# The chunked scan of a hybrid trunk: the state product from two-part operands, and first and last chunks with fewer products

## The chip, the cores and the metric

The kernel runs on one core of a Trainium2 chip. The metric is the device time of one execution in microseconds (us). The engines in the profile are PE (TensorE, matmuls; PEld is its weight load), DVE (VectorE), ACT (ScalarE), POOL (GpSimd) and SP (SyncE, which issues the DMAs).

## The reference

One layer of a trunk over 2048 positions of width 1024, in float32. A normalised input goes through one input projection. Part of its columns feed a short gated convolution, the others a state-space scan (SSD); both are concatenated, projected back and added to the input. A squared-ReLU MLP and a final normalisation follow. The part that matters here is the scan, with 16 heads of 64 in two groups that share B and C (state size 128):

```python
states = einsum("bclgn,bclgrp->bcgrpn", b_c, x_c * decay_end[..., None])
chunk_decay = exp(a_cum[:, :, -1:])
def step(hs, inp):
    s_c, d_c = inp
    return hs * d_c[..., None, None] + s_c, hs
h0 = zeros((b, g, r, p, n))
_, prev = lax.scan(step, h0, (states, chunk_decay))
y_off = einsum("bclgn,bcgrpn->bclgrp", c_c, prev) * exp(a_cum)[..., None]
return y_diag + y_off
...
y = y + d_skip[:, None] * xs
gated = rmsnorm(y * silu(z), norm_w)
```

`y_diag` is the part within a chunk, from scores and decays; `y_off` is what the state before the chunk adds. The state starts at zero, and nobody reads the state after the last chunk.

## The kernel before

The kernel works on chunks of 128 positions. There are 4 blocks `b` of 512 positions, each with 2 groups `g` and 4 chunks `c`: 32 chunks in the order of `CHUNKS`, block by block, group by group. Chunks 0 to 15 (`sp1`, `bufs` of 1) run beside the second half of the input projection (`second_half`, whose matmuls are on lines 267 to 269 into `px`, `py` and `pw`). Chunks 16 to 31 (`sp2`, `bufs` of 2) run beside the output projection (`unit`, whose matmuls are those of `mm3`, lines 110 to 112, into `pm`). After them come the MLP's two projections, which the change does not touch.

The large matmuls already use two-part operands: ACT rounds a tile to float32r (`whi`, line 101; `uh`), DVE subtracts that from the full value (`wlo`, line 102; `ul`), and `mm3` adds up three products hi·hi, hi·lo, lo·hi. The weights `wraw` are loaded by SP (line 96) and split so.

A chunk of the scan goes in these steps.

- `load` and `load_rows`: SP loads B and C (`bc`, line 1184), the inputs `xd` (line 1186), the running decays as rows copied to all partitions (`dec`, line 1188) and their exponentials (`eb`, line 1208). `load_gate` loads `silu(z)` into `y` (line 1215).
- `front`: TensorE transposes `xd` (`ptx`, line 1225) and B (`ptb`, line 1227), and multiplies B and C (line 1228). ACT copies these to `xtok` (line 1230) and `btok` (line 1232); DVE masks the scores (`smask`, line 1234). ACT makes the decays from `dec` (lines 1239 and 1240) and scales `xd` (line 1242). DVE multiplies `xtok` by the steps into `xdt` and by the decays to the chunk's end into `xde` (both line 1245, tile `stmp`), and `dec` by the mask (line 1247).
- `back`: TensorE makes `yo`, the old state by C (line 1259), `st`, the new state product of `btok` and `xde` (line 1261, one fp32 matmul of 128x512), and `yd`, the part within the chunk (line 1264). DVE updates the state (lines 1272 and 1273) and adds up the output (lines 1275 to 1280). A normalisation over the group follows (`ssq`, `pss`, `srstd`, lines 1283 to 1294), and a store to `yn_d` (line 1295).

`front` and `back` are generators. `run` takes their pieces in a written order, and one piece goes after each product of the projection (in `sp1`) or one or two at each hook of a unit (in `sp2`). Each engine executes its queue in order; the queues' order is fixed when the program is built and is not the source's: in the trace an engine has work of the next chunk ahead of work of this one. Every tile waits for the readers of the tile whose buffer it takes over.

Of the kernel before, what the change touches and what calls it, by code (L numbers as in the profile page):

```python
# [11 lines left out]
F32 = mybir.dt.float32  # L12
F32R = mybir.dt.float32r
AF = mybir.ActivationFunctionType
ALU = mybir.AluOpType

P = 128
# [3 lines left out]
NB = T // TB  # L21
L = 128
NC = TB // L
# [16 lines left out]
def trunk(ctx: ExitStack, tc: tile.TileContext, x, w_in, w_dt, w_out, w_up, w_down, cvec, hrow, out):  # L40
    nc = tc.nc
# [67 lines left out]
    def mm3(out, whi, wlo, hi, lo, k, nk):  # L109
        nc.tensor.matmul(out, whi, hi, start=(k == 0), stop=False)  # L110
        nc.tensor.matmul(out, whi, lo, start=False, stop=False)  # L111
        nc.tensor.matmul(out, wlo, hi, start=False, stop=(k == nk - 1))  # L112

    def psum(tag, name, bufs=1):
        if tag in turns:
            tag, bufs = next(turns[tag])
        return ps.tile([P, 512], F32, tag=tag, name=name, bufs=bufs)
# [1029 lines left out]
    class Scan:  # L1147
        def __init__(self, pool):
            self.state = []
            for g in range(G):  # L1150
                s0 = pool.tile([P, 512], F32, name=f"state{g}")
                nc.vector.memset(s0, 0.0)
                self.state.append(s0)

        def open(self, stack, name, bufs):
            self.sp = stack.enter_context(tc.tile_pool(name=name, bufs=1, reuse_waits="tile"))
# [4 lines left out]
            return self.sp.tile([P] + shape, F32, tag=tag, name=tag, bufs=bufs or self.bufs)  # L1161

        def tmp(self):
            return self.tile([512], "stmp", 2 + self.bufs)

        def place(self, n):
            b, g, c = CHUNKS[n]
# [3 lines left out]
        def load(self, n):  # L1171

            if n >= self.end:
                return
            b, g, c, h, ts, r0 = self.place(n)
            t = self.got[n] = {}
            if (g, c) == (0, 0) or n == self.begin:
                dd = self.tile([4, NC * 16], "dd")
                nc.sync.dma_start(dd, dt_d[b])
                self.dd = {**getattr(self, "dd", {}), b: dd}  # L1180
            t["dd"] = dd = self.dd[b]
            bc = t["bc"] = self.tile([2, L], "bc", 2)
            for i in range(2):
                nc.sync.dma_start(bc[:, i], xs_d[h][:, 8 + 2 * i + g, ts])
            t["xd"] = self.tile([4, L], "xd")
            nc.sync.dma_start(t["xd"], xs_d[h][:, 4 * g : 4 * g + 4, ts])
            t["dec"] = self.tile([HG, L], "dec")
            nc.sync.dma_start(t["dec"], rd_d[b][r0 : r0 + HG, 0, :].partition_broadcast(P))
            three = lambda i: dd[:, i].rearrange("p (c h) -> p c h", c=NC)[:, c, g * HG : (g + 1) * HG]
            heads = lambda a: a.unsqueeze(2).to_broadcast([P, HG, 64])  # L1190
            t["dt"], t["cdec"], t["dend"] = heads(three(0)), heads(three(2)), heads(three(3))
            t["a"] = dd[:, 1, r0 : r0 + HG]

        def load_rows(self, n):

            if n >= self.end:
                return
            b, g, c, h, ts, r0 = self.place(n)
            if self.bufs == 1:
                eb = self.tile([4, L], "eb", 1)  # L1200
            else:

                eb = uh.tile([P, 1, TB], F32R, tag="uh3", name="eb", bufs=4).bitcast(F32)
                eb = eb[:, 0].rearrange("p (j l) -> p j l", j=4)
            self.got[n]["eb"] = eb
            for hf in range(2):
                src = rd_d[b][r0 : r0 + HG, 1, :].rearrange("(j t) l -> t j l", t=2)[hf]
                nc.sync.dma_start(eb[hf * 64 : (hf + 1) * 64], src.partition_broadcast(64))

        def load_gate(self, n):  # L1210
# [3 lines left out]
            y = self.got[n]["y"] = self.tile([4, L], "y")  # L1214
            nc.sync.dma_start(y, sz_d[h][:, 4 * g : 4 * g + 4, ts])

        def front(self, n):

            b, g, c, h, ts, r0 = self.place(n)
            t = self.got[n]  # L1220
            bT, cT = t["bc"][:, 0], t["bc"][:, 1]
            byhead = lambda a: a.rearrange("p (h d) -> p h d", h=HG)
            pt = psum("tp", "ptx", 2)
            for j in range(4):
                nc.tensor.transpose(pt[:, j * P : (j + 1) * P], t["xd"][:, j], ident)
            pb = psum("tp", "ptb", 2)
            nc.tensor.transpose(pb[:, 0:P], bT, ident)
            nc.tensor.matmul(pb[:, P : 2 * P], bT, cT, start=True, stop=True)
            xtok = self.tile([512], "xtok", 1)
            nc.scalar.copy(xtok, pt)  # L1230
            btok = t["btok"] = self.tile([P], "btok", 1)
            nc.scalar.copy(btok, pb[:, 0:P])
            sm = self.tile([L], "smask", 1)
            nc.vector.tensor_tensor(out=sm, in0=pb[:, P : 2 * P], in1=tri, op=ALU.mult)
            yield

            dec = t["dec"]
            for i in range(HG):
                nc.scalar.activation(dec[:, i], dec[:, i], AF.Relu, bias=t["a"][:, i : i + 1], scale=-1.0)
            nc.scalar.activation(dec, dec, AF.Exp, scale=-1.0)  # L1240
            for j in range(4):
                nc.scalar.mul(t["xd"][:, j], t["xd"][:, j], col(C_D, 4 * g + j))
            for k, by in (("xdt", "dt"), ("xde", "dend")):
                t[k] = self.tmp()
                nc.vector.tensor_tensor(out=byhead(t[k]), in0=byhead(xtok), in1=t[by], op=ALU.mult)
            yield
            nc.vector.tensor_tensor(out=dec, in0=dec, in1=sm.unsqueeze(1).to_broadcast([P, HG, L]), op=ALU.mult)
            yield

        def back(self, n):  # L1250
# [3 lines left out]
            cT = t["bc"][:, 1]  # L1254
            byhead = lambda a: a.rearrange("p (h d) -> p h d", h=HG)
            state = self.state[g]
            yo = psum("yo", "yo")
            for j in range(4):
                nc.tensor.matmul(yo[:, j * L : (j + 1) * L], state[:, j * P : (j + 1) * P], cT, start=True, stop=True)
            st = psum("tp", "st", 2)  # L1260
            nc.tensor.matmul(st, t["btok"], t["xde"], start=True, stop=True)  # L1261
            yd = psum("yd", "yd")
            for i in range(HG):
                nc.tensor.matmul(  # L1264
# [4 lines left out]
                    stop=True,  # L1269
                )  # L1270
            y = t["y"]
            nc.vector.tensor_tensor(out=byhead(state), in0=byhead(state), in1=t["cdec"], op=ALU.mult)
            nc.vector.tensor_tensor(out=state, in0=state, in1=st, op=ALU.add)
            t1 = self.tmp()
            nc.vector.tensor_tensor(out=t1, in0=yo, in1=t["eb"].rearrange("p j l -> p (j l)"), op=ALU.mult)
            nc.vector.tensor_tensor(out=t1, in0=t1, in1=yd, op=ALU.add)
            yield
            t3 = t1.rearrange("p (j l) -> p j l", j=4)
            nc.vector.tensor_tensor(out=t3, in0=t3, in1=t["xd"], op=ALU.add)
            nc.vector.tensor_tensor(out=y, in0=t3, in1=y, op=ALU.mult)  # L1280
            yield
            q4 = self.tmp().rearrange("p (j l) -> p j l", j=4)
# [4 lines left out]
            yield  # L1287
            pss = psum("tp", "pss", 2) if self.bufs == 1 else psum("mw", "pss", accs["mw"])
            nc.tensor.matmul(pss[:, 0:L], ones, ssq, start=True, stop=True)
            r = self.tile([L], "srstd", 1)  # L1290
            nc.scalar.activation(r, pss[:, 0:L], AF.Sqrt, bias=eps, scale=1.0 / 512)
            nc.vector.reciprocal(out=r, in_=r)
            yield
# [339 lines left out]
```

## Time and profile before

| | |
|---|---|
| time of 3 runs | 2644.2, 2649.08, 2650.53 us; median 2649.08 |
| profiled execution | span 2642.3 us from the first to the last instruction; the page gives it no other time |
| engines busy | PE 98%, PEld 80%, DVE 74%, ACT 54%, POOL 2% |
| granted TensorE clock | 0.998 on average |
| scan's first product to its last | about 480 to 1280 us |

A line of a timeline reads: start in us from the span's beginning, duration, engine (SPq is SP's queue), line of the code, operation, output<-inputs, shapes, how many in a row; in brackets the idle time of the engine before it and what ended it. A line of a group reads: line, engine, operation, tiles, shapes and count, then busy us and mean ns of one, then the idle time before them. A line of a wait reads: who waited <- for whom: us in total, times, the longest. Matmuls are pipelined, so that their durations overlap; the distance from start to start is what one occupies.

### The profile page before, as it was taken

Reading aid. Unit: us, or ns where it says so; the run is one execution under the profiler, and the core shown is the slowest. Engines: PE = TensorE matmul, PEld = TensorE weight load, DVE = VectorE, ACT = ScalarE, POOL = GpSimd, SP = SyncE. Lnnn points to the kernel's source line nnn. Section 1 sums busy time; section 2 is a strip of 40 time slices with the busy share of each in tenths; the row PEclk is TensorE's granted clock in tenths of the full one; section 3 lists DMA queues with packets and bytes.
Section 4 is the critical chain, followed back from the end, with each engine's and each line's share of the span. In section 5 each row is a group of like instructions: output and inputs, shape, how many; then the busy total and the mean of one; then the engine's idle time right before and its main releaser. Section 6 shows DMA issues by size and latency. Waiting matters only on the chain.

```text
span 2642.3 us, 33439 instructions
## 1 busy us (share of the span) xinstructions
PE 2595.5 (98%) x12026; PEld 2121.3 (80%) x12026; DVE 1943.0 (74%) x2650; ACT 1423.9 (54%) x2150; POOL 57.4 (2%) x98
## 2 busy tenths in 40 slices
PE   7999999999999999999999999999999999999998
PEld 5778888778878888887888888788887888888887
DVE  7987676767777777758777775755558877888885
ACT  6644345777567666657326555755455444444443
POOL 0000010000000000000000000000000000000001
PEclk9999999999999999999999999999999999999999
DMA  3585444655555479967666673743448544665762
GB/s 146 192 304 187 143 144 174 205 160 168 158 167 186 153 242 273 288 205 233 212 210 215 227 277 142 250 162 140 166 144 299 160 149 153 211 209 175 243 207 72
DMA packets 284806, 511.78 MB, mean 194 GB/s; under 512 B 25312, under 2 KB 141024, under 8 KB 284640
## 3 DMA queue, kind: packets, MB, share of 16 engines
q1 hardware_dynamic: 284640, 509.65, 57.9%
q8 instruction: 94, 1.54, 0.2%
q14 instruction: 72, 0.59, 0.1%
HBM read 344.41 MB, written 165.15 MB: 193 GB/s over the span
## 4 chain that ended last, share of the span: by engine, by line
PE 64%; issue 24%; DMA 4%; ACT 3%; DVE 3%; SPq 1%; POOL 0%; POOLq 0%; DVEq 0%; ACTq 0%
PE px L267 9%; PE px L269 9%; PE px L268 9%; PE py L267 5%; PE py L269 5%; PE py L268 4%; PE pm L110 4%; PE pm L111 4%; PE pm L112 4%; PE pw L267 2%; PE pw L268 2%; PE pw L269 2%; DMA dec<-rd_d 2%; PE yd L1264 1%; PE st L1261 1%
## 5 line engine op out<-in xcount | busy, mean ns | idle before, releaser
L267 PE MATMUL px<-uh,whi 128*128 128x512 f32 x1672 | 656.9, 393 | 7.8 <-ACT pw L275 3.9
L269 PE MATMUL px<-uh,wlo 128*128 128x512 f32 x1672 | 652.0, 390 | 2.5 <-DVE wlo L102 2.5
L268 PE MATMUL px<-ul,whi 128*128 128x512 f32 x1672 | 651.9, 390 | 0.0
L102 DVE TENSOR_TENSOR wlo<-wraw,whi 128x1024 fp32r<-128x1024 f32 x230 | 233.8, 1017 | 212.0 <-ACT whi L101 203.1
L267 PEld LDWEIGHTS px<-uh,whi 128*128 128x128 f32 x1672 | 314.3, 188 | 82.7 <-DVE acc L984 7.0
L269 PEld LDWEIGHTS px<-uh,wlo 128*128 128x128 f32 x1672 | 314.3, 188 | 69.4 <-DVE wlo L102 3.3
L268 PEld LDWEIGHTS px<-ul,whi 128*128 128x128 f32 x1672 | 314.3, 188 | 63.6
L101 ACT CAST whi<-wraw 128x1024 fp32r<-128x1024 f32 x230 | 203.3, 884 | 278.3 <-PE px L268 198.0
L101 ACT CAST whi<-s 128x1024 fp32r<-128x1024 f32 x210 | 219.3, 1044 | 234.5 <-PE py L268 76.2
L267 PE MATMUL py<-uh,whi 128*128 128x512 f32 x836 | 327.3, 392 | 1.9 <-DVE acc L984 1.5
L268 PE MATMUL py<-ul,whi 128*128 128x512 f32 x836 | 325.5, 389 | 0.0
L269 PE MATMUL py<-uh,wlo 128*128 128x512 f32 x836 | 325.4, 389 | 0.0
L102 DVE TENSOR_TENSOR wlo<-s,whi 128x1024 fp32r<-128x1024 f32 x210 | 255.6, 1217 | 82.6 <-ACT whi L101 78.9
L110 PE MATMUL pm<-uh,whi 128*128 128x512 f32 (+1 forms) x648 | 251.8, 390 | 2.1 <-ACT uh L202 2.1
L111 PE MATMUL pm<-ul,whi 128*128 128x512 f32 (+1 forms) x648 | 248.9, 384 | 0.0
L112 PE MATMUL pm<-uh,wlo 128*128 128x512 f32 (+1 forms) x648 | 248.3, 383 | 0.0
L267 PEld LDWEIGHTS py<-uh,whi 128*128 128x128 f32 x836 | 157.0, 188 | 35.9 <-DVE acc L984 1.9
L269 PEld LDWEIGHTS py<-uh,wlo 128*128 128x128 f32 x836 | 156.9, 188 | 32.8
L268 PEld LDWEIGHTS py<-ul,whi 128*128 128x128 f32 x836 | 157.0, 188 | 32.3 <-issue 0.2
L267 PE MATMUL pw<-uh,whi 128*128 128x512 f32 x418 | 163.4, 391 | 0.7 <-ACT pw L275 0.7
L268 PE MATMUL pw<-ul,whi 128*128 128x512 f32 x418 | 162.8, 390 | 0.0
L269 PE MATMUL pw<-uh,wlo 128*128 128x512 f32 x418 | 162.8, 389 | 0.0
(226 smaller groups left out, 3671.1 us busy)
## 6 DMA issues: line engine op xcount, KB each, us to landing
hid_d<-e SPq DMA_DIRECT2D x96, 512.0 KB, 3.6
rh<-hid_d SPq DMA_DIRECT2D x96, 512.0 KB, 4.4
wraw<-w_in SPq DMA_DIRECT2D x68, 512.0 KB, 4.0
wraw<-w_up SPq DMA_DIRECT2D x64, 512.0 KB, 4.3
wraw<-w_down SPq DMA_DIRECT2D x104, 256.0 KB, 3.7
dec<-rd_d SPq DMA_DIRECT2D x32, 512.0 KB, 5.6
wraw<-w_out SPq DMA_DIRECT2D x32, 512.0 KB, 5.1
x_d<-xt SPq DMA_DIRECT2D x64, 256.0 KB, 3.8
```

The costliest lines, as they stand in the source:

```text
L101: nc.scalar.copy(hi, raw)
L102: eng.tensor_tensor(out=lo, in0=raw, in1=hi.bitcast(F32), op=ALU.subtract)
L110: nc.tensor.matmul(out, whi, hi, start=(k == 0), stop=False)
L111: nc.tensor.matmul(out, whi, lo, start=False, stop=False)
L112: nc.tensor.matmul(out, wlo, hi, start=False, stop=(k == nk - 1))
L267: nc.tensor.matmul(p, hi, h[0], start=bool(first and k == 0), stop=False, **kw)
L268: nc.tensor.matmul(p, hi, h[1], start=False, stop=False, **kw)
L269: nc.tensor.matmul(p, lo, h[0], start=False, stop=(k == len(g) - 1), **kw)
L1261: nc.tensor.matmul(st, t["btok"], t["xde"], start=True, stop=True)
L1264: nc.tensor.matmul(yd[(i % 2) * 64 : (i % 2) * 64 + 64, (i // 2) * L : (i // 2 + 1) * L], byhead(t["xdt"])[:, i, :], t["dec"][:, i, :], st ...
```

## The change

The state product `st` is made by `mm3` from two-part operands: a helper `pieces` lets ACT round the source to float32r (`hi`) and DVE subtract (`lo`). `btok` is split straight from PSUM in the place of its copy; `xde` is now computed in place in `xtok` and split from there. The first chunk of each group (`b` and `c` zero) leaves out `yo` and the load of `eb`; its state is a copy of `st` in the place of an update of a zeroed tile. The last chunk of each group leaves out the transpose of B, `btok`, `xde`, `st` and the state's update. The rotating tile `stmp` has one buffer fewer, and `r` takes the tile of `ssq`.

```diff
             for g in range(G):
-                s0 = pool.tile([P, 512], F32, name=f"state{g}")
-                nc.vector.memset(s0, 0.0)
-                self.state.append(s0)
+                self.state.append(pool.tile([P, 512], F32, name=f"state{g}"))
...
         def tmp(self):
-            return self.tile([512], "stmp", 2 + self.bufs)
+            return self.tile([512], "stmp", 1 + self.bufs)
...
+            t["first"], t["last"] = (b, c) == (0, 0), (b, c) == (NB - 1, NC - 1)
...
         def load_rows(self, n):
...
+            if self.got[n]["first"]:
+                return
...
+        def pieces(self, shape, tag, src):
+            pair = self.sp.tile([P] + shape, F32R, tag=tag, name=tag, bufs=1)
+            hi, lo = pair[:, 0], pair[:, 1]
+            nc.scalar.copy(hi, src)
+            nc.vector.tensor_tensor(out=lo, in0=src, in1=hi.bitcast(F32), op=ALU.subtract)
+            return hi, lo
 
         def front(self, n):
...
-            nc.tensor.transpose(pb[:, 0:P], bT, ident)
+            if not t["last"]:
+                nc.tensor.transpose(pb[:, 0:P], bT, ident)
...
-            btok = t["btok"] = self.tile([P], "btok", 1)
-            nc.scalar.copy(btok, pb[:, 0:P])
+            if not t["last"]:
+                t["btok"] = self.pieces([2, P], "btok", pb[:, 0:P])
...
-            for k, by in (("xdt", "dt"), ("xde", "dend")):
-                t[k] = self.tmp()
-                nc.vector.tensor_tensor(out=byhead(t[k]), in0=byhead(xtok), in1=t[by], op=ALU.mult)
+            t["xdt"] = self.tmp()
+            nc.vector.tensor_tensor(out=byhead(t["xdt"]), in0=byhead(xtok), in1=t["dt"], op=ALU.mult)
+            if not t["last"]:
+                nc.vector.tensor_tensor(out=byhead(xtok), in0=byhead(xtok), in1=t["dend"], op=ALU.mult)
+                t["xde"] = self.pieces([2, 512], "xde", xtok)
...
         def back(self, n):
...
-            yo = psum("yo", "yo")
-            for j in range(4):
-                nc.tensor.matmul(yo[:, j * L : (j + 1) * L], state[:, j * P : (j + 1) * P], cT, start=True, stop=True)
-            st = psum("tp", "st", 2)
-            nc.tensor.matmul(st, t["btok"], t["xde"], start=True, stop=True)
+            if not t["first"]:
+                yo = psum("yo", "yo")
+                for j in range(4):
+                    nc.tensor.matmul(yo[:, j * L : (j + 1) * L], state[:, j * P : (j + 1) * P], cT, start=True, stop=True)
+            if not t["last"]:
+                st = psum("tp", "st", 2)
+                mm3(st, *t["btok"], *t["xde"], 0, 1)
...
-            nc.vector.tensor_tensor(out=byhead(state), in0=byhead(state), in1=t["cdec"], op=ALU.mult)
-            nc.vector.tensor_tensor(out=state, in0=state, in1=st, op=ALU.add)
             t1 = self.tmp()
-            nc.vector.tensor_tensor(out=t1, in0=yo, in1=t["eb"].rearrange("p j l -> p (j l)"), op=ALU.mult)
-            nc.vector.tensor_tensor(out=t1, in0=t1, in1=yd, op=ALU.add)
-            yield
             t3 = t1.rearrange("p (j l) -> p j l", j=4)
-            nc.vector.tensor_tensor(out=t3, in0=t3, in1=t["xd"], op=ALU.add)
+            if t["first"]:
+                nc.vector.tensor_copy(state, st)
+                yield
+                nc.vector.tensor_tensor(out=t1, in0=yd, in1=t["xd"].rearrange("p j l -> p (j l)"), op=ALU.add)
+            else:
+                if not t["last"]:
+                    nc.vector.tensor_tensor(out=byhead(state), in0=byhead(state), in1=t["cdec"], op=ALU.mult)
+                    nc.vector.tensor_tensor(out=state, in0=state, in1=st, op=ALU.add)
+                nc.vector.tensor_tensor(out=t1, in0=yo, in1=t["eb"].rearrange("p j l -> p (j l)"), op=ALU.mult)
+                nc.vector.tensor_tensor(out=t1, in0=t1, in1=yd, op=ALU.add)
+                yield
+                nc.vector.tensor_tensor(out=t3, in0=t3, in1=t["xd"], op=ALU.add)
...
-            r = self.tile([L], "srstd", 1)
+            r = ssq
```

## The prediction

> **What bounds the kernel now.** I read the page first: how full each engine is, and what the chain of the last-ending work consists of.
>
> ```profile
> span 2642.3 us, 33439 instructions
> PE 2595.5 (98%) x12026; PEld 2121.3 (80%) x12026; DVE 1943.0 (74%) x2650; ACT 1423.9 (54%) x2150; POOL 57.4 (2%) x98
> ...
> PEclk9999999999999999999999999999999999999999
> ...
> PE px L267 9%; PE px L269 9%; PE px L268 9%; PE py L267 5%; PE py L269 5%; PE py L268 4%; PE pm L110 4%; PE pm L111 4%; PE pm L112 4%; PE pw L267 2%; PE pw L268 2%; PE pw L269 2%; DMA dec<-rd_d 2%; PE yd L1264 1%; PE st L1261 1%
> ```
>
> TensorE is busy for 98% of the span at full clock, and the chain runs almost wholly through its matmuls, a little through the scan's load of `dec`. So time taken off TensorE is time gained, if nothing makes it wait instead. The scan runs as side work of two stages: chunks 0 to 15 beside the input projection, 16 to 31 beside the output projection. The sums by window, and TensorE's waits within them:
>
> ```profile
> 480.00:974.00 494.00, 488.70 (x2428) 392.67 (x2428) 362.97 (x504) 338.64 (x563) 16.55 (x38) 1.00 0.55 172
> 974.00:1290.00 316.00, 314.51 (x1658) 253.92 (x1657) 225.46 (x345) 190.23 (x377) 0.00 (x0) 1.00 0.80 246
> ...
> PE yd L1264 <- DVE dec L1247: 3.2, 3, 1.7
> ...
> PE st L1261 <- DVE stmp L1245: 0.4, 1, 0.4
> ```
>
> After the length of each window come PE, PEld, DVE and ACT busy. Together DVE has 588.4 of 810 us and ACT 528.9, so both have room; in the second stage the DMA share is 0.80, and TensorE is idle for only 1.5 us of 316.
>
> The result is counted from the median, 2649.08. The profile gives its execution's span, 2642.3, without a time of its own; the three runs lie 1.9 to 8.2 us above that span and the median 6.8. I work out the change against the span and put it on the median. 0.3%, about what a measurement of this kernel can tell from no change, is 7.9 us: faster is below 2641.1, slower above 2657.0.
>
> **The state product on TensorE.** TensorE's timeline over one chunk, whose product is cut at the window's edge so that both its halves show, and the transposes of another:
>
> ```profile
> 1015.67 0.39 PE L112 MATMUL pm<-uh,wlo 128*128 128x512 f32 x1
> ...
> 1016.35 0.39 PE L112 MATMUL pm<-uh,wlo 128*128 128x512 f32 x1
> 1016.58 1.05 PE L1259 MATMUL yo<-bc,state 128*128 128x128 f32 x8
> 1017.47 1.02 PE L1261 MATMUL st<-stmp,btok 128*128 128x512 f32 x2
> ...
> 1017.90 0.59 PE L1261 MATMUL st<-stmp,btok 128*128 128x512 f32 x1
> ...
> 1018.42 0.55 PE L1264 MATMUL yd<-dec,stmp 128*64 128x128 f32 x6
> ...
> 1008.05 0.27 PE L1227 MATMUL ptb<-ident,bc 128*128 128x128 f32 x1
> 1008.16 0.39 PE L1228 MATMUL ptb<-bc 128*128 128x128 f32 x2
> ...
> L267 PEld LDWEIGHTS py<-uh,whi 128*128 128x128 f32 x836 | 157.0, 188 | 35.9 <-DVE acc L984 1.9
> ```
>
> Ends overlap the next start, so starts are what to subtract. A split-operand matmul takes (1016.58 - 1015.67) / 4 = 0.2275 us. The fp32 product is two instructions: 0.43 to the second start and 0.52 from there to `yd`, of which 0.09 over the first's 0.43 goes with the turn to `yd`'s 128*64 form. After: 3 x 0.2275 = 0.68, and the same 0.09; weight loads of 0.188 fit under a pass. That is 0.95 - 0.77 = 0.18 a chunk, in the 30 chunks that keep the product: 5.4 us.
>
> [...]
>
> **The products left out.** A `yo` takes 1017.47 - 1016.58 = 0.89; the two first chunks, 0 and 4, lose it. The last chunks, 27 and 31, lose the product (0.86 without the turn) and the transpose of B (8.16 - 8.05 = 0.11): 2 x 0.97 = 1.9. Sum of everything: 5.4 + 1.8 + 1.9 = 9.1. But where TensorE waits for `dec` right afterwards, work removed ahead of it only makes the wait longer:
>
> ```profile
> 491.25 1.09 PE L1264 MATMUL yd<-dec,stmp 128*64 128x128 f32 x16 [1.15 <-DVE dec L1247]
> ...
> 556.53 1.09 PE L1264 MATMUL yd<-dec,stmp 128*64 128x128 f32 x16 [1.66 <-DVE dec L1247]
> ```
>
> These are chunks 0 and 2. I strike 0.89 + 2 x 0.18 = 1.2 and keep 7.9 us.
>
> **The splits on DVE and ACT.** Groups by shape, over both stages:
>
> ```profile
> L101 ACT CAST whi<-a 128x512 fp32r<-128x512 f32 x20 | 12.3, 616 | 10.6 <-PE px L268 10.5
> ...
> L102 DVE TENSOR_TENSOR wlo<-a,whi 128x512 fp32r<-128x512 f32 x20 | 13.7, 685 | 3.9 <-ACT whi L101 3.9
> ...
> L1234 DVE TENSOR_TENSOR smask<-ptb,tri 128x128 f32<-128x128 f32 x32 | 9.2, 286 | 3.7 <-ACT btok L1232 3.7
> ...
> L1272 DVE TENSOR_TENSOR state<-state,dd 128x512 f32<-128x512 f32 x32 | 22.0, 686 | 5.3 <-PE yo L1259 5.3
> ```
>
> A chunk gains a rounding of `xde` on ACT (0.616, as `whi` of that shape) and two subtractions on DVE: 0.685 for `xde` and, from PSUM like `smask`, 0.286 for `btok`. The rounding of `btok` replaces a copy. Over 30 chunks: ACT +18.5, DVE +29.1. The four edge chunks give back about a dozen DVE operations of the size of the `state` row, some 8 us. DVE goes to about 610 of 810 us, 75%, ACT to 68%; neither becomes the bound. The `eb` loads of two chunks, the memsets, and `r` in the place of `ssq` I cost at nothing: no wait of TensorE names any of them. One slot fewer of `stmp` goes with one allocation fewer a chunk, so each slot is still reused by work that has ended by then.
>
> What counts is the added latency: the product must now wait for product by `dend` (DVE), rounding (ACT), subtraction (DVE). In the first stage there is room, in the second little:
>
> ```profile
> 713.93 0.68 DVE L1245 TENSOR_TENSOR stmp<-xtok,dd 128x512 f32<-128x512 f32 x1
> ...
> 727.30 1.02 PE L1261 MATMUL st<-stmp,btok 128*128 128x512 f32 x2
> ...
> 1164.67 0.68 DVE L1245 TENSOR_TENSOR stmp<-xtok,dd 128x512 f32<-128x512 f32 x1
> 1165.27 1.22 DVE L1247 TENSOR_TENSOR dec<-dec,smask 128x1024 f32<-128x1024 f32 x1
> ...
> 1166.41 0.69 DVE L1459 TENSOR_TENSOR xt<-pm,xt 128x512 f32<-128x512 f32 x1
> ...
> 1166.99 1.02 PE L1261 MATMUL st<-stmp,btok 128*128 128x512 f32 x2
> ...
> 1184.67 1.09 PE L1261 MATMUL st<-stmp,btok 128*128 128x512 f32 x2
> ...
> 1223.49 0.69 DVE L1245 TENSOR_TENSOR stmp<-xtok,dd 128x512 f32<-128x512 f32 x1
> ...
> 1224.33 1.10 PE L1261 MATMUL st<-stmp,btok 128*128 128x512 f32 x2 [0.40 <-DVE stmp L1245]
> ```
>
> Chunk 8 has 727.30 - 714.61 = 12.7 us to spare: hidden. Chunk 26 has 1166.99 - 1165.35 = 1.6. There I expect 0.2 more for `btok`'s low part, then the product with `dec`, 1.14 to the next start, under which ACT rounds, then 0.69: 2.0, which is 0.4 late. Chunk 29 has 0.15, so 1.9 late. Behind a late product TensorE holds `yd` and the output projection; behind the rounding ACT holds the next chunk's `dec` and `whi`, behind the low part DVE holds the eviction `xt`. Bounds: nothing (TensorE's order may put other matmuls ahead; the 0.4 of today may go too), and 4.5, an estimate: four chunks like 26 lose 0.4 each, chunk 29 1.9, one between them 1.0. I take 1.9, chunk 29's, the only product that waits already. 7.9 - 1.9 = 6.0: **2643.1**, between 2639.6 (9.1 and the 0.4) and 2645.7 (7.9 - 4.5).
>
> **Rival 1, slower: the splits lengthen a loop that runs beside TensorE.** The queues over one chunk of the second stage:
>
> ```profile
> 1163.27 0.56 ACT L1230 COPY xtok<-ptx 128x512 f32<-128x512 f32 x1
> ...
> 1168.33 1.03 ACT L101 CAST whi<-wraw 128x1024 fp32r<-128x1024 f32 x1
> 1169.39 1.23 DVE L102 TENSOR_TENSOR wlo<-wraw,whi 128x1024 fp32r<-128x1024 f32 x1 [2.29 <-ACT whi L101]
> ...
> 1170.64 0.33 SPq L96 DMA_DIRECT2D wraw<-w_out  x1
> ...
> 1173.13 0.56 SPq L1188 DMA_DIRECT2D dec<-rd_d  x1
> ...
> 1174.81 0.60 PE L1225 MATMUL ptx<-ident,xd 128*128 128x128 f32 x4
> ...
> 1180.65 1.58 ACT L1239 ACTIVATE dec<-dec,dd 128x128 f32<-128x128 f32 x5 [3.84 <-DMA dec<-rd_d]
> ...
> 1182.43 0.56 ACT L1230 COPY xtok<-ptx 128x512 f32<-128x512 f32 x1
> ```
>
> ACT's copy of `xtok` follows 7.6 us after the transposes, because the next chunk's `dec` stands ahead of it and waits for its load; that load stood in SP's queue behind the load of `wraw`, issued when `wlo` ended; `wlo` waited for ACT's `whi`. From copy to copy that is 19.16 us, while TensorE goes from product to product in 1184.67 - 1166.99 = 17.68: this turn used up 1.5 of the slack. New ACT and DVE work ahead of `whi` and `wlo` adds 0.62 + 0.69, with `btok` 1.5, to each turn. It decides from the point where the slack is below that: then TensorE pays it each chunk. The last 11 of the stage's products make 16.5, and a load that misses its turn at SP costs more. 16.5 - 7.9 = 8.6 slower, 2657.7; at 2.5 a chunk 2668. Likely value 2660. For it: the chain names `dec<-rd_d`. Against: `wlo` is in the loop only in some turns, and a late TensorE gives slack back. [...]
>
> **Rival 2: no gain from three passes.** Between two fp32 neighbours a turn to split operands and back might cost 0.09 twice more, all of the 0.18. Left are 2.9 (7.9 less 28 x 0.18), less 1.9: 1.0, so 2648.1. Against: `yo` starts 0.23 after the split matmul before it, so the turn into fp32 costs nothing.
>
> **How the numbers follow.** Forecast 0.66, rival 1 0.26, rival 2 0.08. Of the forecast 0.38 lies below 2641.1 (no wait added: the removed work counts in full) and 0.28 above. Faster 0.38, same 0.28 + 0.08 = 0.36, slower 0.26. The forecast's own range is 2638 to 2646. For 8 in 10 the range goes up to 2660, which leaves out half of rival 1, and down to 2637, for waits that vanish with a new order.
>
> **What would show it.** Right: three `st` matmuls at 0.23 and about 0.77 from the first to `yd`; no `yo` in chunks 0 and 4; TensorE's idle time in 974 to 1290 at 2 to 6 us, its waits named `st` on DVE. Wrong: waits of `st` or `yd` in nearly every chunk from 20 on, `xtok` over 8 us behind `ptx` (rival 1), or a `st` of 0.95 (rival 2). DVE above 80% there would break the whole count.

## The result, and the profile after

The changed kernel takes 2650.32 us (median of 13 runs, 2644.07 to 2654.08); the kernel before takes 2649.08 (13 runs, 2644.20 to 2652.89). The ratio is 1.0002, with a 95% interval of 0.9993 to 1.0010: no change that this measurement can tell. The profiled execution took 2651.74 us, with a span of 2649.9. By the 1.8 us between these two, the profiled execution of the kernel before, with a span of 2642.3, was the shortest of its 13 runs, so the 7.5 us between the spans are not the difference between the kernels.

The page of the kernel after, its lines that answer to those of before:

```profile
span 2649.9 us, 33529 instructions
PE 2594.9 (98%) x12034; PEld 2128.0 (80%) x12034; DVE 1958.4 (74%) x2696; ACT 1431.7 (54%) x2174; POOL 54.6 (2%) x98
...
PE px L267 9%; PE px L269 9%; PE px L268 9%; PE py L269 4%; PE py L267 4%; PE py L268 4%; PE pm L110 4%; PE pm L111 4%; PE pm L112 4%; PE pw L267 2%; PE pw L269 2%; PE pw L268 2%; DMA dec<-rd_d 1%; PE yd L1278 1%; PE yo L1272 1%
```

By this page little happened: the state product is gone from the end of the chain's list, TensorE's sum of busy time is the same, and DVE's and ACT's are 15 and 8 us larger. The two windows, and TensorE's waits within the second, show more (after the length: PE, PEld, DVE, ACT and POOL busy, then the granted clock, the DMA share and GB/s):

```profile
480.00:974.00 494.00, 490.42 (x2451) 397.65 (x2450) 371.99 (x531) 340.59 (x576) 14.50 (x38) 1.00 0.56 173
974.00:1290.00 316.00, 307.99 (x1628) 252.00 (x1627) 230.22 (x364) 195.50 (x387) 0.00 (x0) 0.98 0.78 239
```
```profile
PE st L110 <- ACT xde L1222: 7.8, 2, 4.0
```

In the second window TensorE is idle for 8.0 us in place of 1.5, the granted clock is 0.98 in place of 1.00, and one wait has taken the place of the small ones: the state product waits twice, 7.8 us together, for ACT's rounding of `xde`. In both TensorE stands still; the first one in its timeline:

```profile
1106.95 1.05 PE L1272 MATMUL yo<-bc,state 128*128 128x128 f32 x8
1111.97 0.79 PE L110 MATMUL st<-xde,btok 128*128 128x512 f32 x1 [3.97 <-ACT xde L1222]
1112.69 0.80 PE L111 MATMUL st<-xde,btok 128*128 128x512 f32 x1
1113.29 0.63 PE L112 MATMUL st<-xde,btok 128*128 128x512 f32 x1
1113.85 1.98 PE L1278 MATMUL yd<-dec,stmp 128*64 128x128 f32 x16
1115.75 0.80 PE L110 MATMUL pm<-uh,whi 128*128 128x512 f32 x1
```

This is chunk 23; chunk 29 has the other, 3.85 us up to 1228.53. Without a stop a chunk takes 2.70 us from the start of `yo` to the next large matmul (637.77 to 640.47 in the view after the next); here it takes 1115.75 - 1106.95 = 8.80, and 8.68 at chunk 29. That is 6.1 and 6.0 us more, and only 4.2 of it lies ahead of the product's start (1111.97 - 1106.95, in place of 0.80). The rest is nearly all the clock, by windows around the stop:

```profile
1100.00:1106.00 6.00, 6.00 (x28) 4.98 (x27) 3.88 (x7) 1.74 (x6) 0.00 (x0) 1.00 0.86 252
1106.00:1112.00 6.00, 2.03 (x14) 1.64 (x13) 3.68 (x8) 5.97 (x15) 0.00 (x0) 0.91 0.84 261
1112.00:1116.00 4.00, 4.00 (x20) 2.58 (x21) 3.75 (x6) 0.86 (x1) 0.00 (x0) 0.50 0.97 317
1116.00:1120.00 4.00, 4.00 (x16) 3.25 (x17) 2.23 (x4) 1.93 (x3) 0.00 (x0) 0.78 0.86 276
```

The granted clock is 0.50 for 6.8 us: 1.1 us before 1112 (0.09 x 6 / 0.50), the 4 us behind it and 1.8 us more (0.22 x 4 / 0.50). The sixteen `yd` take 1.90 to the next start, and with the full clock they take 1.02. The half clock goes on for 2.0 us behind the next large matmul's start, which costs another 1.0: some 7.1 us in all for this stop, and 6.7 by the same count for the one at chunk 29.

Where the removed work should be, it is. A chunk of the first stage, in the same view:

```profile
637.77 1.05 PE L1272 MATMUL yo<-bc,state 128*128 128x128 f32 x8
638.57 0.48 PE L110 MATMUL st<-xde,btok 128*128 128x512 f32 x1
638.89 0.40 PE L111 MATMUL st<-xde,btok 128*128 128x512 f32 x1
639.12 0.40 PE L112 MATMUL st<-xde,btok 128*128 128x512 f32 x1
639.45 1.09 PE L1278 MATMUL yd<-dec,stmp 128*64 128x128 f32 x16
640.47 0.50 PE L267 MATMUL py<-uh,whi 128*128 128x512 f32 x1
...
610.28 0.39 PE L110 MATMUL st<-xde,btok 128*128 128x512 f32 x1
...
611.05 1.09 PE L1278 MATMUL yd<-dec,stmp 128*64 128x128 f32 x16
```

The last two rows are chunk 4, which has no `yo` any more: its product takes 611.05 - 610.28 = 0.77, as forecast. After a `yo` the first pass takes 0.32 and `yo` 0.80 in place of 0.89, so `yo` and `st` go from 1.84 to 1.68: 0.16 a chunk for the 0.18 of the forecast.

The two stages, cut at TensorE's first matmul of the next stage, tell it in two numbers of one execution each. From the start of the input projection's second half to its last product, beside chunks 0 to 15, the time goes from 503.9 to 499.6 us; from there to the MLP's first matmul, beside chunks 16 to 31, from 417.2 to 425.9.

### The profile page after: what moved, and what is told of

Same layout as the page of the kernel before. It is cut to its first block, busy times and chain, and to the rows that moved or that the text cites. A ratio compares the mean times of both kernels' runs of the same rounds, so it can differ in the third digit from the quotient of the medians.

```text
span 2649.9 us, 33529 instructions
## 1 busy us (share of the span) xinstructions
PE 2594.9 (98%) x12034; PEld 2128.0 (80%) x12034; DVE 1958.4 (74%) x2696; ACT 1431.7 (54%) x2174; POOL 54.6 (2%) x98
## 4 chain that ended last, share of the span: by engine, by line
PE 64%; issue 25%; DMA 4%; ACT 4%; DVE 3%; SPq 1%; POOL 0%; POOLq 0%; DVEq 0%; ACTq 0%
PE px L267 9%; PE px L269 9%; PE px L268 9%; PE py L269 4%; PE py L267 4%; PE py L268 4%; PE pm L110 4%; PE pm L111 4%; PE pm L112 4%; PE pw L267 2%; PE pw L269 2%; PE pw L268 2%; DMA dec<-rd_d 1%; PE yd L1278 1%; PE yo L1272 1%
## 5 line engine op out<-in xcount | busy, mean ns | idle before, releaser
L267 PE MATMUL px<-uh,whi 128*128 128x512 f32 x1672 | 656.4, 393 | 10.8 <-ACT pw L275 4.1
L317 ACT CAST uh<-rh 128x1024 fp32r<-128x1024 f32 (+1 forms) x128 | 120.3, 943 | 79.6 <-PE py L269 61.7
```

What stands on the lines that cost most here:

```text
L267: nc.tensor.matmul(p, hi, h[0], start=bool(first and k == 0), stop=False, **kw)
L317: nc.scalar.copy(p[i][0], t)
```

## The experiments

All were run in alternation with the kernel before, whose medians in the four batches were 2646.12, 2645.74, 2645.86 and 2645.34 us. Times are medians; the interval is of the ratio to the kernel before. "Stages" are the two lengths just given, "wait" is the longest wait of a state product in the profiled execution, and "clock" is the granted clock averaged over all runs of the kernel (0.9973 to 0.9976 for the kernel before in the four batches), which tells of the stops in executions that were not traced. A length and a wait are those of one execution, which can be far from the median: e10's took 2645.90 us, e12's 2655.46.

| kernel | us | ratio, interval | stages | wait | clock |
|---|---|---|---|---|---|
| before (the first profile) | 2649.08 | 1 | 503.9, 417.2 | 0.4 | see above |
| e0 after, again | 2646.18 | 0.9991, 0.9981 to 1.0001 | 497.9, 420.4 | 2.5 | 0.9959 |
| e1 edges alone | 2647.16 | 0.9992, 0.9980 to 1.0005 | 502.1, 427.5 | 6.1 | 0.9972 |
| e2 passes alone | 2654.80 | 1.0023, 1.0012 to 1.0034 | 504.9, 426.8 | 4.8 | 0.9962 |
| e3 rounding on DVE | 2648.81 | 1.0012, 1.0001 to 1.0024 | 500.3, 425.0 | 4.3 | 0.9955 |
| e5 a fourth `xt` | 2646.66 | 1.0004, 0.9996 to 1.0013 | 498.1, 423.9 | 6.8 | 0.9961 |
| e6 before, a fourth `xt` | 2649.19 | 1.0018, 1.0006 to 1.0030 | 503.6, 420.7 | 0.7 | 0.9974 |
| e7 no low parts | 2642.48 | 0.9991, 0.9981 to 1.0001 | 497.4, 420.0 | 3.4 | 0.9964 |
| e8 e5 and e3 | 2648.74 | 1.0012, 1.0002 to 1.0022 | 498.8, 424.7 | 7.0 | 0.9958 |
| e9 whole chain on DVE | 2644.31 | 0.9993, 0.9983 to 1.0003 | 499.4, 424.2 | 5.5 | 0.9963 |
| e10 before, chain on DVE | 2652.65 | 1.0025, 1.0014 to 1.0036 | 504.9, 418.7 | 0.2 | 0.9971 |
| e11 `dec` loaded by POOL | 2672.51 | 1.0102, 1.0089 to 1.0115 | 497.0, 451.3 | 5.6 | 0.9922 |
| e12 fills spread | 2647.40 | 1.0009, 0.9999 to 1.0019 | 501.6, 425.9 | 5.5 | 0.9962 |

**The change again, and its two parts.** e0 is the kernel after, unchanged. e1 has only the work left out of first and last chunks, with the fp32 product; e2 has only the split operands and three passes, in all 32 chunks.

> The changed kernel once more, to see whether what its profile shows is there each time. Theory W (waits): ACT's queue is fixed, and in chunks 23 and 29 the rounding of xde stands behind the rest of the next chunk's decays and their exponential; so TensorE stops again between yo and st there, 3 to 5 us each, and the clock drops to half after it. Ratio to before 0.999 to 1.002. Rival L (load): the 20 us of added DVE work slow many places a little; then the two stops are a chance of that run and are mostly gone, with the ratio still near 1.000.

> Only the first and last chunks' left-out work; the state product stays one fp32 matmul, with the copy of btok and four or three slots of stmp as before. W and L both: 2 x 0.89 for yo and 2 x 0.97 for st and the transpose of B make 3.7, of which chunk 0's 0.89 may go into a wait: 2.8 to 3.7 us faster, ratio 0.9986 to 0.999. No wait of st on ACT. If it is not faster, removed TensorE work does not count here at all.

> Only the three-pass product with its splits, in all 32 chunks; no chunk leaves anything out. W: yo, st and yd together take 2.82 in place of 2.98, so 32 x 0.16 = 5 us faster if nothing waits; each chunk in which ACT's rounding of xde stands behind the exponential of the next chunk's decays costs up to 6 us, so 2644 with none, 2656 with two. The difference from 2644 should be the sum of such stops. L: 2650 or more with no single wait of st above 1 us.

The core of e1 and of e2 against the kernel before:

```diff
 e1
+            if not t["first"]:
                 yo = psum("yo", "yo")
...
+            if not t["last"]:
                 st = psum("tp", "st", 2)
                 nc.tensor.matmul(st, t["btok"], t["xde"], start=True, stop=True)
 e2
-            nc.tensor.matmul(st, t["btok"], t["xde"], start=True, stop=True)
+            mm3(st, *t["btok"], *t["xde"], 0, 1)
```

The same program gives other sizes of the two stops each time: in e0's profiled execution the first waits 2.5 us and the second hardly 0.5, so a single span of this kernel can't be compared closer than some us. What varies less is the clock: e0 has 0.995 to 0.997 in its 11 runs, the kernel before 0.997 or 0.998 in nearly all. 0.9973 - 0.9959 = 0.0014 of 2646 us is 3.7 us lost to a lower clock; at a granted 0.50 that is 7.4 us spent at half speed, about one stretch like the one of 6.8 us shown, or two short ones. The first 13 runs have 0.9960 on average. So by the clock a run of the kernel after has about one such stop more than a run of the kernel before, not two; single runs differ, and 0.997 occurs with both kernels. Half clock in the MLP is in this figure too. The first profile of each of the two kernels has 3.4 us of it there, but in e0's the clock from 1290 to 2640 us is 0.99 where both of these have 1.00, so part of the difference may lie there.

The passes make them frequent: e2 has 0.996 or 0.997 throughout and is slower than the kernel before. e1 has 0.997 or 0.998 in ten of twelve runs; its profile, with a wait of 6.1 us at chunk 29, is of its longest run, 2654.51 us at 0.995. It says little of the others, but it shows that such a stop needs no passes. The parts don't quite add: 0.9992 and 1.0023 would make 1.0015 together, and e0 has 0.9991, the first measurement of the same kernel 1.0002; with intervals of 0.001 on each side that is at the edge of the noise. Part of it is seen in the first stage, which e2 doesn't shorten at all (504.9): small waits for ACT appear there, the largest that of the normalisation's product:

```profile
PE pss L1297 <- ACT xtok L1238: 2.6, 4, 1.2
```

**The rounding moved to DVE (e3).** In the timeline of the kernel after the cause of the first stop reads like a plain queueing fault. ACT around it:

```profile
1104.26 0.41 ACT L1249 ACTIVATE dec<-dec,dd 128x128 f32<-128x128 f32 x1 [6.49 <-DMA dec<-rd_d]
1104.57 0.62 ACT L1303 ACTIVATE stmp<-y 128x512 f32<-128x512 f32 x1
...
1105.97 0.57 ACT L1240 COPY xtok<-ptx 128x512 f32<-128x512 f32 x1
...
1107.48 1.56 ACT L1249 ACTIVATE dec<-dec,dd 128x128 f32<-128x128 f32 x5
1109.06 1.28 ACT L1250 ACT_TABLE_LOAD   x1
1110.36 1.06 ACT L1250 ACTIVATE dec<-dec 128x1024 f32<-128x1024 f32 x1
1111.32 0.60 ACT L1222 CAST xde<-xtok 128x512 fp32r<-128x512 f32 x1
```

ACT waits 6.49 us for chunk 24's `dec`, and chunk 23's copy of `xtok` stands behind it. Then the rest of chunk 24's decays, a table load and the exponential, 3.8 us, still stand ahead of chunk 23's rounding, for which TensorE waits. At chunk 26 the same rounding starts at 1167.05, ahead of the exponential, and nothing stops. e3 takes the rounding out of that queue:

```diff
-                t["xde"] = self.pieces([2, 512], "xde", xtok)
+                t["xde"] = self.pieces([2, 512], "xde", xtok, nc.vector.tensor_copy)
```

> The changed kernel with xde rounded by DVE in place of ACT, so that the chain from xtok to st no longer goes through ACT's queue; DVE gets some 0.4 to 0.7 us a chunk more, ACT 0.6 less. W: the stops are gone, no wait of st above 1 us, 8 to 10 us faster than before: 2639 to 2641, ratio 0.996 to 0.997. L: DVE is loaded with 10 to 20 us more than in the changed kernel, so 2650 or slower, ratio 1.000 or above.

It isn't that alone: the waits are now on DVE's rounding and are 2.4 and 4.3 us long,

```profile
PE st L110 <- DVE xde L1222: 6.7, 2, 4.3
```

and the clock over its runs is 0.9955. What ACT waits for first is the load. In the kernel after chunk 24's `dec` lands at 1104.15, 13.0 us behind the start of chunk 22's `yd`, and the product of chunk 23 waits 4.0. In e3 it lands 14.2 us behind it, and the product waits 2.4. So the new place gives chunk 23 some 2.7 us more room, but the load is later. At chunk 29 the place is worth 0.2: the load lands 12.5 us behind chunk 28's `yd` in the kernel after, for a wait of 3.9, and 13.2 in e3, for one of 4.3. The rounding is the last link of the stop, not its start.

**A fourth buffer for the residual (e5, e6, e8).** SP issues the load of `dec` in order, behind a load of `xt` that waits for the store of the tile whose buffer it takes over. A fourth `xt` should let it pass (`stmp` gives up the room):

```diff
-            return self.tile([512], "stmp", 1 + self.bufs)
+            return self.tile([512], "stmp", 2)
...
-                t = self.xt[n] = self.xp.tile([P, TB], F32, tag="xt", name="xt", bufs=3)
+                t = self.xt[n] = self.xp.tile([P, TB], F32, tag="xt", name="xt", bufs=4)
```

e6 is the same in the kernel before, without the line of `stmp`; e8 is e5 with e3's rounding.

> The changed kernel with four buffers of xt in place of three (stmp has two in both stages to make room). Theory S (SP's loop): beside the output projection a turn store of xt, landing, load of xt, load of dec, decays on ACT, copy of xtok, st takes as long as TensorE's own chunk, so any shortening of TensorE's work ends as a stop near chunks 23 and 29, and half the clock after it. With a buffer more, SP no longer waits for the store: dec is issued within 4 us of yd, no wait of TensorE for st above 2 us, 2637 to 2642, ratio 0.996 to 0.998. Theory P (the splits' latency alone): the chain through ACT and DVE is as long as ever; still stops of 3 to 5 us, ratio 0.999 to 1.001.

> The kernel before with four buffers of xt, as a control. S: its loop is just as long as TensorE's chunk, with little waited for, so the buffer brings 0 to 3 us: ratio 0.999 to 1.000. P: no change. If it gains as much as the changed kernel does from the same buffer, the buffer is a gain of its own and says nothing of the change.

> Four buffers of xt, and xde rounded by DVE in place of ACT, otherwise the changed kernel: both suspects relieved. S: as with the buffer alone, 2636 to 2641, the rounding's place makes under 2 us. P: better than the buffer alone by 4 us or more.

The product of chunk 23 waits for no rounding in e5 any more, and the wait at chunk 29 grows to 6.8 us; e8 has 7.0 there. Both follow the load. Chunk 24's `dec` now lands 8.7 us behind the start of chunk 22's `yd` in place of 13.0, as was wanted; chunk 30's lands 15.5 behind chunk 28's in place of 12.5, and there SP still waits for stores of `xt` ahead of its loads (6.3 us in two waits between 1196 and 1213). So the lever worked at one chunk and not at the other. Nothing is won in sum, and the kernel before gets slower by the same buffer.

**No low parts (e7).** Three passes over the rounded parts alone: no rounding on ACT for `xde` (DVE's multiply writes it rounded) and no subtractions on DVE. It tells the splits' own work from the shorter product.

```diff
-                nc.vector.tensor_tensor(out=byhead(xtok), in0=byhead(xtok), in1=t["dend"], op=ALU.mult)
-                t["xde"] = self.pieces([2, 512], "xde", xtok)
+                hi = self.sp.tile([P, 512], F32R, tag="xde", name="xde", bufs=1)
+                nc.vector.tensor_tensor(out=byhead(hi), in0=byhead(xtok), in1=t["dend"], op=ALU.mult)
+                t["xde"] = hi, hi
```

> The changed kernel without the low parts: DVE's product by dend writes xde rounded, ACT's copy writes btok rounded, and the three passes use the high parts three times, so that TensorE does the same work and neither ACT nor DVE has anything added (the low parts' terms are left out of the result). xt has three buffers. P: without the splits nothing waits, 2637 to 2641, ratio 0.996 to 0.9975. S: the loop through SP is still there, stops near chunks 23 and 29 remain in most runs as they do with the edges alone: 2643 to 2648, ratio 0.998 to 1.000.

Without any of the splits' work behind the multiply a wait of 3.4 us remains at chunk 29, the clock is 0.9964, and the ratio 0.9991 is that of e0. So a stop doesn't need the rounding and the subtractions. They do matter: in e7 chunk 30's `dec` lands 15.8 us behind chunk 28's `yd`, 3.4 later than in the kernel after, and the wait is shorter all the same, where e5 and e8, at 15.5 and 15.9, wait 6.8 and 7.0.

**The whole chain on DVE (e9, e10).** ACT's copies of `xtok` and `btok` go too: DVE multiplies straight from PSUM and rounds. e10 does the same to the kernel before.

```diff
-            nc.scalar.copy(hi, src)
+            nc.vector.tensor_copy(hi, src)
...
-            nc.scalar.copy(xtok, pt)
...
-            nc.vector.tensor_tensor(out=byhead(t["xdt"]), in0=byhead(xtok), in1=t["dt"], op=ALU.mult)
+            nc.vector.tensor_tensor(out=byhead(t["xdt"]), in0=byhead(pt), in1=t["dt"], op=ALU.mult)
```

> The changed kernel with everything between the transposes and the state product on DVE: xdt and xde are multiplied straight from PSUM, without ACT's copy to xtok, and DVE rounds both btok and xde. Theory A (ACT's queue holds the chain): in the second stage ACT stands at the next chunk's decays, waiting for the load of dec, and everything of this chunk that ACT has to do waits with it, xtok in both kernels and the roundings in the changed one; the buffer of xt did not matter since dec's load stands behind other things at SP too. Off ACT, the load may come 10 us later without harm: no wait of TensorE for st or yd above 1 us beside the output projection, the clock stays at 1.00, the stage from the projection's end to the MLP falls to 414 or less, 2636 to 2641, ratio 0.995 to 0.998. Rival L (load): DVE has some 35 us more than before, so waits on DVE and 2650 or slower.

> The kernel before with the same chain on DVE: xdt and xde from PSUM, btok copied by DVE, no xtok. A: the kernel before waits little here by its profile, but in its slower runs the same stops should be in it; 0 to 4 us faster, ratio 0.9985 to 1.000; then the changed kernel with the chain on DVE is 5 to 9 us ahead of it, which is the removed TensorE work. L: slower by 1 to 4 us.

Now no instruction of ACT lies between the transposes and the product. The wait at chunk 23 falls to 1.4 us, the one at chunk 29 is 5.5. In that stretch, DVE's and then ACT's timeline of e9 (the multiply of `xdt` at the end of the first part is the first link of the chain, 12.7 us behind its transposes at 1209.4):

```profile
1211.20 1.23 DVE L102 TENSOR_TENSOR wlo<-wraw,whi 128x1024 fp32r<-128x1024 f32 x1 [2.43 <-ACT whi L101]
1213.42 0.95 DVE L1311 RECIPROCAL ssq<-ssq 128x128 f32<-128x128 f32 x1 [0.99 <-ACT ssq L1310]
...
1219.27 0.42 DVE L1303 TENSOR_TENSOR stmp<-stmp 128x256 f32<-128x256 f32 x1 [1.03 <-ACT stmp L1302]
...
1221.24 0.69 DVE L1493 TENSOR_TENSOR facc<-sq,facc 128x512 f32<-128x512 f32 x1 [1.16 <-ACT sq L1492]
...
1222.06 0.68 DVE L1253 TENSOR_TENSOR stmp<-ptx,dd 128x512 f32<-128x512 f32 x1
```
```profile
1208.90 1.33 ACT L1412 ACTIVATE uh<-ry,cv 128x512 fp32r<-128x512 f32 x2 [4.67 <-DMA ry<-yn_d]
...
1216.85 1.87 ACT L1248 ACTIVATE dec<-dec,dd 128x128 f32<-128x128 f32 x6 [3.46 <-DMA dec<-rd_d]
```

DVE waits four times for ACT, 5.6 us in all, for work that has nothing to do with the product (weights, the normalisation, the residual's squares); and ACT had waited 4.67 and 3.46 us for two DMAs. Taking the chain off ACT moves the wait one engine on; chunk 30's `dec` lands at 1216.8, 14.3 us behind chunk 28's `yd`. The pair is of use in another way: with this chain on DVE in both, the change is worth 2652.65 - 2644.31 = 8.3 us between the medians, and the intervals of the two ratios (up to 1.0003, from 1.0014) don't meet. That is about the 9.1 us of work that the change removes, but e10 is a slowed-down kernel before, so it isn't a gain. Where e10 loses its time isn't shown, since its profiled execution took 6.8 us less than its median.

**Later loads of `dec` (e11).** POOL, which has little else to do, issues the second stage's loads of `dec`, in two halves. That was to bring them earlier; as it turned out they come later, which makes it the opposite lever.

```diff
-            nc.sync.dma_start(t["dec"], rd_d[b][r0 : r0 + HG, 0, :].partition_broadcast(P))
...
+                for i in range(2):
+                    nc.gpsimd.dma_start(t["dec"][:, 4 * i : 4 * i + 4], rows[4 * i : 4 * i + 4].partition_broadcast(P))
```

> The changed kernel with the loads of dec of the second stage issued by the idle POOL queue, in two halves, in place of SP's; the chain through ACT stays. A and the loop through SP: dec is issued within 1 us of yd of two chunks before, ACT's decays do not wait for it, no stop above 2 us: 2637 to 2642, ratio 0.996 to 0.998, unless the issue by POOL takes longer than SP's wait (over 8 us from yd to landing in 13 us), in which case the stops stay. L: no change, 0.999 to 1.001.

The waits between 974 and 1320 us:

```profile
ACT dec L1254 <- DMA dec<-rd_d: 59.1, 19, 7.0
...
PE st L110 <- ACT xde L1227: 20.7, 6, 5.6
```

ACT's wait for `dec` is longer than the 39.9 us that the kernel after has between 974 and 1290, and the product waits six times in place of twice, 1.3 to 5.6 us each; the stage takes 25.4 us more than in the kernel after. More delay of that load makes more stops of the same kind. ACT's sum of waits alone doesn't tell a stop: the kernel before has 36.4 us of the same waits and none.

**The output projection's fills spread (e12).** In both chunks that stop, a four-part fill of the output projection's operands (eight instructions on ACT, `uh`, eight on DVE, `ul`) runs too; others, from 1071.7 and 1188.2 on, go by without a stop. The hooks that call two of them were moved apart:

```diff
-            put(1, 0, 1, 34, (38, 40, 42, 44))
+            put(1, 0, 1, 34, (40, 46, 52, 56))
...
-            put(1, 2, 0, 68, (72, 74, 76, 78))
+            put(1, 2, 0, 68, (72, 78, 84, 88))
```

> The kernel after, with two of the output projection's four-part fills (lines 1413 and 1414, eight instructions on ACT and eight on DVE each) spread over three chunks in place of one: hooks 40, 46, 52, 56 for 38, 40, 42, 44, and 72, 78, 84, 88 for 72, 74, 76, 78. In the trace of after these sixteen instructions run at 1085 to 1103 and 1204 to 1219 us, in the periods of chunks 23 and 29, the two that stop TensorE, and load ACT there by 5.7 and DVE by 6.0 us of a chunk's 17.5. Theory F (the removed product is given back where the loop beside TensorE carries a fill as well): the stops after 1107 and 1224 us go or fall under 1 us each, the part beside the output projection falls from 425.9 to 412 to 417 us, xtok comes at most 6.5 us behind ptx in chunks 23 and 29; time 2633 to 2641 us, ratio 0.995 to 0.998. Rival D (DMA loads of dec that come late hold ACT, fills or not): ACT still waits 5 to 6 us for dec in one line and the stops stay at these chunks or move to others, 3 to 7 us each; ratio 0.9985 to 1.0005.

The first of those fills, in ACT's timeline of the kernel after and then of e12:

```profile
1091.97 2.55 ACT L1413 ACTIVATE uh<-ry,cv 128x512 fp32r<-128x512 f32 x4
...
1095.37 0.72 ACT L1413 ACTIVATE uh<-ry,cv 128x512 fp32r<-128x512 f32 x1
```
```profile
1090.80 3.77 ACT L1413 ACTIVATE uh<-ry,cv 128x512 fp32r<-128x512 f32 x6
...
1095.42 0.72 ACT L1413 ACTIVATE uh<-ry,cv 128x512 fp32r<-128x512 f32 x1
```

The lever didn't move: all eight still start between 1087 and 1096, now even closer together: where the hook stands in the source did not decide their place in ACT's queue. So e12 tests neither theory; as one more kernel of nearly the same order it stops at the same two chunks, for 2.9 and 5.5 us.

## Why the prediction was right or wrong

The forecast was 2643.1 us with a range of 2637 to 2660, and chances of similar size for faster, same and slower. The kernel came out at 2650.32: in the range, in the case "within 0.3%", 7 us above the number. The forecast's own range, 2638 to 2646, is missed. That the wide one holds the result is luck in part: its upper end was drawn for rival 1, whose toll in every chunk did not come.

- **The removed work** was sized right. A chunk's product, 0.95 before, is 0.77 without `yo` ahead of it, as forecast; with `yo` the saving is 0.16 for 0.18. `yo` is gone from chunks 0 and 4. The 1.2 us struck for chunks 0 and 2 needn't have been: in the kernel after no `yd` waits for `dec` in the first stage. The eight profiled kernels that have both parts and SP's loads of `dec` take 497.4 to 501.6 us for the first stage, 499.1 on average; the three without either part 503.6 to 504.9, 504.1 on average. The gain there is 5.0 us, about the 4.7 worked out for it (16 products of 0.18 and two `yo` of 0.89).
- **The costs at nothing** held. DVE has 602 of 810 us for the 610 forecast, ACT 536 at 66% for 68%, and neither is the bound by its share.
- **The waits added, 1.9 us with bounds of 0 and 4.5, are the term that was mis-sized.** By the same two groups of kernels the second stage takes 423.8 on average in place of 418.9: 4.9 us more, where about 4.2 us of work were taken out (14 products of 0.16, 2 x 0.97 for the last chunks). So some 9 us are given back there, twice the upper bound, in profiled executions. Of these the three without either part lie 2.9 to 6.8 us below their kernels' medians, and the others 1.4 above on average, so some us of it may be chance. The clock over all runs gives a second estimate: a mean lower by 0.0014, 3.7 us, is about one stop a run like the one of chunk 23, which lost 3.4 by its 6.8 us at half clock and 7.1 in all. In the kernel after's own profile it is 425.9 - 417.2 + 4.2 = 12.9: the two stops of 7.1 and 6.7, less about 1 us of small waits that the kernel before has.
- **Two steps of its working failed.** It took the slack of the kernel before as given: a chunk loses what that slack lacks, tenths of a us in a few chunks. The stops are rare and whole; chunk 26 has none, chunk 23, which was not on the list, loses as much as chunk 29. The load of `dec` moved too, as shown below. And it priced a stop at its wait. The half clock behind it adds more than half as much again, 7.1 us for a wait of 4.0. So its sign of being right, TensorE idle for 2 to 6 us in the second window with waits of `st` on DVE, did not come: 8.0 us, and waits on ACT.
- **Rival 1 had the mechanism in part**: work of the next chunk, waiting for its `dec`, holds ACT, and the copy of `xtok` starts 8.0 and 8.5 us behind `ptx` at chunks 23 and 29. The 8 that was named as its sign separates little: the kernel before reaches 7.9, at chunk 28, without a stop. It was wrong on the rest. It isn't a toll in every chunk, and a loop lengthened by the splits' work isn't needed: e7 leaves that out and stops all the same.
- **Rival 2** fell: the passes cost 0.77.

What sets the length of a stop can be read from the traces. Take the time from the start of chunk 28's `yd` to the landing of chunk 30's `dec`, where ACT's wait for it ends. In the kernel after this is 1220.3 - 1207.8 = 12.5 us:

```profile
1220.30 1.57 ACT L1249 ACTIVATE dec<-dec,dd 128x128 f32<-128x128 f32 x5 [5.34 <-DMA dec<-rd_d]
```

Chunk 29's product then waits, in us:

| kernels | the load lands after | the product waits | difference |
|---|---|---|---|
| splits, rounding on ACT: e0, after, e2, e12, e5 | 8.9, 12.5, 13.5, 14.1, 15.5 | 0.3, 3.9, 4.8, 5.5, 6.8 | 8.6 to 8.7 |
| splits, rounding on DVE: e3, e9, e8 | 13.2, 14.3, 15.9 | 4.3, 5.5, 7.0 | 8.8 |
| without the splits' work on `xde`: before, e6, e7, e1 | 11.2, 11.8, 15.8, 18.2 | 0.4, 0.7, 3.4, 6.1 | 10.8 to 12.5 |

(e10, without splits, has 13.2 and no wait; e11 loads in halves.) So the product waits for as long as the load is late beyond a fixed room, and the splits take 2 to 4 us of that room; the prediction had worked out 2.0 of added latency. At chunk 23 the same holds with a room of 9.1 for after, e0, e2 and e12. What the prediction lacked is that the load doesn't stay where it was. At chunk 23 it lands 13.0 and 11.5 us behind that `yd` in the two executions of the kernel after, in place of 10.5; at chunk 29 12.5 and 8.9, in place of 11.2. In e7 and e1, which have the larger room, it is later still, and the room is used up again.

What the runs show of the cause, and what not. Shown, in the profiled executions: the gain is kept in the first stage and given back in the second; it goes in stops of TensorE at chunk 23, 29 or both, whose length follows the lateness of the next chunk's `dec`, and in the half clock with them; by the clock, the kernels with the three passes have up to about one more of them a run than the kernel before. Neither the rounding's engine, nor ACT's part of the chain, nor the low parts, nor a buffer of `xt` is the cause by itself. What sets the time of the load isn't shown. An explanation is argued: beside the output projection the side work runs at TensorE's pace already (in the kernel before, chunk 29's `yd` starts 0.06 us after its last operand is made, chunk 27's 0.05), held by SP's, ACT's and DVE's waits for one another and for loads, so that any time taken off TensorE there comes back as a wait. A direct test would be a kernel that speeds that loop up by itself, and none of these did at both chunks. Whether the two fills at chunks 23 and 29 decide where it breaks stays open, since e12 did not move them.

None of the kernels is clearly faster than the one before; e9, with 0.9993, is not.

## What to carry to other kernels

Count a stage's slack before counting what work removed from TensorE is worth in it: here a dependent loop ended within 0.1 us of its use, and a saving of 0.2 us per turn brought nothing in that stage in any of the kernels. Price a stop of TensorE above its own length (here 7.1 us for a wait of 4.0), and read the granted clock of all runs: by its means, 0.9959 and 0.9973, the half clock took more time in one kernel than in the other, which one traced execution of each could not tell. When the same stop has another length in each trace, look for the event whose lateness varies with it. And when a lever is moved in the source, look in the trace whether the instructions moved.

## What the runs showed of the hardware

In these traces TensorE's clock falls to half with waits as short as 1.86 us, and the length alone doesn't decide. A wait of 1.37 us (e9, chunk 23) left it at 1.00; one of 2.50 (e0, chunk 23), that of 3.97 (the kernel after, chunk 23) and one of 5.5 (e9, chunk 29) each brought it to 0.50:

```profile
1104.00:1108.00 4.00, 1.50 (x11) 1.24 (x9) 2.40 (x4) 3.97 (x7) 0.00 (x0) 0.93 0.88 274
1108.00:1112.00 4.00, 4.00 (x20) 2.58 (x20) 3.75 (x6) 0.58 (x1) 0.00 (x0) 0.50 1.00 330
```

The rows are e0's. In the kernel after's trace a wait of 1.86 us in the MLP (the matmul into `px` at 1704.66) is followed by 0.50 from 1705 to 1708, and one of 2.62 (into `py` at 2026.77) by 1.00 from 2027 to 2031. The kernel before has one such half clock too, 0.50 from 1700 to 1703, after a wait of 2.08 us. By windows of 1 us the half clock lasts 3.4 us in each of these two places of the MLP and 6.8 at chunk 23. So here a wait of 1.86 us was enough, and one of 2.62 was not.

In the kernel before an fp32 product of 128x512 took 0.43 us to the start of its second instruction and 0.52 from there to `yd`, and a float32r one 0.2275. In the kernel after the first pass behind the fp32 `yo` took 0.32, 0.09 more than 0.23, and `yo` 0.80 in place of 0.89.

ACT kept the order of its queue in the stop of chunk 23: it stood idle for the 6.49 us up to 1104.26, waiting for chunk 24's `dec`, though chunk 23's `ptx`, begun at 1097.98, was there to be copied; the copy came at 1105.97.

Runs of the same kernel, on the same chip, spread by up to 0.7% (e1, 2636.51 to 2654.51), more than the whole change removes.
